# Two steps of the state-space units go from VectorE and GpSimd to ScalarE

## The chip, the cores and the metric

The kernel runs on one core of one Trainium2 chip, as one program. The metric is device microseconds of that core for one execution. Times in the traces are microseconds from the start of the span unless a duration is marked ns. Engines are named as the profile names them: PE (TensorE matmul), PEld (its weight loads), DVE (VectorE), ACT (ScalarE), POOL (GpSimd), SP (the queue that issues most of the transfers).

## The reference, cut to what matters

One layer over 1024 latent tokens and 256 context tokens: a token mixer (differential attention beside a bidirectional Mamba-2 scan, merged by gates), then a mixture of experts. The change touches only the scan. In its chunked form, for one direction:

```python
acum = jnp.cumsum(dtc * a, axis=2)
seg = acum[:, :, :, None] - acum[:, :, None]
decay = jnp.where(lower, jnp.exp(jnp.where(lower, seg, 0.0)), 0.0)
cb = jnp.einsum('bcign,bcjgn->bcijg', cc, bc)
y_diag = jnp.einsum('bcijg,bcijgr,bcjgr,bcjgrp->bcigrp', cb, decay, dtc, xc)
y_off = jnp.einsum('bcign,cbgrpn,bcigr->bcigrp', cc, h_prev, jnp.exp(acum))
```

The kernel does both directions together with chunks of 128 tokens. For each head it needs a matrix W of 128 rows (j) by 128 columns (i) for each chunk: the mask "j up to i" times dt forward plus the mask "j from i" times dt backward, times exp of the smaller of the two differences of the running sums, times the product of B and C.

## The kernel before, in words

The program is built in stages: norm and attention's projections (to about 390 us), the mixer `mixer_t` (about 390 to 1050), attention with the branch products in its gaps, the merge, the experts. A planner written in the kernel (`Flow`) sets the order of all instructions of PE, DVE, ACT and POOL. Each piece of work is a generator (a stream) with a priority, lower first; at each `yield` it names what it needs next: tiles, free buffers of a ring, and the engine whose planned clock must be reached (`wake`, L294). Where no engine is named, the engine is PE. The planner charges a cost for each instruction and hands it to its engine in the order in which streams wake. The engines then run their queues in order and wait for each other by semaphores.

In the mixer, `server` (L945, priority 3) feeds PE with the projections: for each output tile of 128 channels ("job") it multiplies split weights `hi`, `lo` with the normalised tokens into `acc` banks, and goes back to the planner after nine matmuls of 512 columns or at a job's end (six more). Jobs are dt, convolution inputs, z and 16 gate tiles; gate tiles need no scan and are taken when the others can't run. `mixer_load` (L777) fetches a job's weights, ACT casts them to `hi`, DVE subtracts to `lo`.

`dt_post` (L826) makes `dt` and the running sums `ac` (partition j, by direction, chunk and head), and stores their rows to DRAM (`acd`). For each of four head groups, `group` (L990) makes transposes, the `states` of both directions (L1048), and four pairs of units. A **unit** (L1078) is one head over half of the tokens (four chunks); a pair is two heads of the same half. The unit fetches rows of `acd` into two tiles R (one per direction, broadcast over partitions), gets a G and a W buffer, and then:

- DVE: W = mask le times dt, four instructions of 128 by 128 (`F.ts`, one scalar by partition); then W = mask ge times the other dt plus W, four more (`F.stt`)
- POOL: G = R[0] minus the column of `ac`, one instruction of 128 by 512 (`F.ptt`), after R[0] has landed
- DVE: G = min(R[1] minus its column, G), four instructions
- `decays` (L1127): ACT takes exp of R[0] and R[1] in place, POOL multiplies each by C
- POOL: W = W times the product of B and C (`CB`); ACT: exp of G; DVE: W = W times G

`products` (L1111) waits until both units of a pair are planned and their tiles are 400 ns old, then gives PE the matmuls of both heads into `py`, and frees R and W. The rings hold six R, two G and two W. So both W of a pair are in use until its products ran, and the next pair's units start then; one unit's R are fetched ahead, the other's when the products free theirs. After the fourth pair `norm` (L1151) normalises the group's output and stores it (`yn`).

When the fourth group is done, the branch products (`branches`, L1194) open: they load `yn`, and attention's first tiles (`qk`) are fetched once no job is left and five operands are in. Both must come before attention's first matmuls (`sps`).

Of the kernel before, what the change touches and what calls it, by code (L numbers as in the profile page):

```python
# [13 lines left out]
AF = mybir.ActivationFunctionType  # L14
ALU = mybir.AluOpType
# [4 lines left out]
P = 128  # L20
# [354 lines left out]
class Layer:  # L375
# [413 lines left out]
    def mixer_t(s):  # L789
        tc, nc, I, F = s.tc, s.nc, s.I, s.F  # L790
# [9 lines left out]
        if True:  # L800
# [15 lines left out]
            Gs = s.ring(sp, [P, 4, P], "G", 2)  # L816
            Ws = s.ring(sp, [P, 4, P], "W", 2)
            dcol, db = s.dcol, s.db
            dtn = mp.tile([P, 2, 10, 32], F32, name="dtn")
            dt, dtd = dtn[:, 0], dtn[:, 1]  # L820
            ac = mp.tile([P, 2, 10, 16], F32, name="ac")
            cdec = mp.tile([P, 10, 2, 16], F32, name="cdec")
            wst = mp.tile([P, 10, 2, 16], F32, name="wst")
            state = {"dt": False, "conv": {}, "z": set(), "groups": 0, "served": False}

            def dt_post(banks):  # L826
                yield [db, "ACT"]
                F.act(db[:, 1], db[:, 1], AF.Exp)
                yield [aux]
                pt = aux.get()  # L830
                for b, t0, n in zip(banks, (L, L + 512, 0), (512, 512, L)):
                    yield [b, Gs, "ANY"]
                    q = Gs.get()
                    qv = q.rearrange("p a b -> p (a b)")
                    F.copy(qv[:64, :n], b[:64, :n])
                    acc.put(b)
                    yield [q]
                    for i in range(n // P):
                        c = t0 // P + i
                        F.mm(pt[:, c * 32:(c + 1) * 32], q[:64, i], s.fold[:64], True, True)  # L840
                    Gs.put(q)
                yield [pt, db, (Gs, 2), "DVE"]
                tiles = Gs.get(), Gs.get()
                u, e = (q.rearrange("p a b -> p (a b)")[:, :320] for q in tiles)
                F.tt(u.rearrange("p (c h) -> p c h", h=32), pt[:, :320].rearrange("p (c h) -> p c h", h=32), db[:, 0:1].to_broadcast([P, 10, 32]), ALU.add)
                aux.put(pt)
                yield [u, "ACT"]
                F.act(e, u, AF.Abs)
                F.act(e, e, AF.Exp, scale=-1.0)
                F.act(e, e, AF.Ln, bias=1.0)  # L850
                yield [e, "DVE"]
                F.stt(dt.rearrange("p c h -> p (c h)"), u, 0.0, e, ALU.max, ALU.add)
                Gs.put(*tiles)
                yield [dtn, "DVE"]
                F.stt(dtd, dt, -1.0, db[:, 1:2].to_broadcast([P, 10, 32]), ALU.mult, ALU.mult)
                for d, tri in ((0, s.le), (1, s.ge)):
                    yield [dtn, aux]
                    pa = aux.get()
                    F.mm(pa[:, :160].rearrange("p (c h) -> p c h", h=16), tri, dtd[:, :, d * 16:(d + 1) * 16], True, True)
                    yield [pa, "DVE"]  # L860
                    F.vcopy(ac[:, d].rearrange("p c h -> p (c h)"), pa[:, :160])
                    aux.put(pa)
                yield [aux]
                pt = aux.get()
                F.mm(pt[:, :320], s.ones, dtd.rearrange("p c h -> p (c h)"), True, True)
                yield [pt, "ACT"]
                F.act(cdec.rearrange("p c d h -> p (c d h)"), pt[:, :320], AF.Exp)
                yield [ac, "DVE"]
                F.tt(wst, pt[:, :320].rearrange("p (c d h) -> p c d h", d=2, h=16), ac.rearrange("p d c h -> p c d h"), ALU.subtract)
                aux.put(pt)  # L870
                wf = wst.rearrange("p c d h -> p c (d h)")
                yield [wst, "ACT"]
                F.act(wf.rearrange("p c h -> p (c h)"), wf.rearrange("p c h -> p (c h)"), AF.Exp)
                yield [wst, "DVE"]
                F.tt(wf, wf, dt, ALU.mult)
                for d, tri in ((0, s.le), (1, s.ge)):
                    for half in range(2):
                        yield [aux]
                        pa = aux.get()
                        for c in range(4):  # L880
                            F.mm(pa[:16, c * P:(c + 1) * P], dtd[:, 2 + half * 4 + c, d * 16:(d + 1) * 16], tri, True, True)
                        yield [pa, Gs, "DVE"]
                        q = Gs.get()
                        qv = q.rearrange("p a b -> p (a b)")
                        F.vcopy(qv[:16], pa[:16])
                        aux.put(pa)
                        F.dma(s.acd[d][:, half * 512:(half + 1) * 512], qv[:16])
                        Gs.put(q)
                state["dt"] = True
# [55 lines left out]
            def server():  # L945
                box = s.mbox
                nxt = pick()
                while nxt:
# [35 lines left out]
                    if kind == "dt":  # L984
                        F.spawn(0, dt_post(banks))
                    elif kind == "conv":
                        F.spawn(0, conv_post(q, v, 0 if q >= 12 else L, banks))
                state["served"] = True

            def group(g, x0, x1, B, C):  # L990
# [40 lines left out]
                for pair in range(2):  # L1031
                    for half in range(2):
                        yield [pys]
                        py, ready = pys.get(), []
                        for hh in range(2):
                            yield [(Rs, 2), "NOW"]
                            F.spawn(0, unit(g, pair, half, hh, CB, C, ready))
                        F.spawn(1, products(g, pair, half, xn, hp, py, done, ready, yt))
# [39 lines left out]
            def unit(g, pair, half, hh, CB, C, ready):  # L1078

                r = 2 * pair + hh  # L1080
                h = 4 * g + r
                t0 = 512 * half
                R = [Rs.get(), Rs.get()]
                for d in range(2):
                    F.dma(R[d], bass.AP(tensor=s.acd[d].tensor, offset=s.acd[d].offset + h * T + t0, ap=[[0, P], [1, 512]]))
                Rv = [q.rearrange("p (c i) -> p c i", i=P) for q in R]
                yield [Gs, Ws, "DVE"]
                G, W = Gs.get(), Ws.get()
                cs = range(4 * half, 4 * half + 4)
                for c in range(4):  # L1090
                    F.ts(W[:, c], s.le, dt[:, 2 + cs[c], h:h + 1], None, ALU.mult)
                for c in range(4):
                    F.stt(W[:, c], s.ge, dt[:, 2 + cs[c], 16 + h:16 + h + 1], W[:, c], ALU.mult, ALU.add)
                yield [R[0], "POOL"]
                F.ptt(G, Rv[0], ac[:, 0, 2 + 4 * half:6 + 4 * half, h:h + 1].to_broadcast([P, 4, P]), ALU.subtract)
                yield [G, R[1], "DVE"]
                for c in range(4):
                    F.stt(G[:, c], Rv[1][:, c], ac[:, 1, 2 + cs[c], h:h + 1], G[:, c], ALU.subtract, ALU.min)
                k = []
                F.spawn(0, decays(R, C[:, t0:t0 + 512], k, F.clk["DVE"] + 100.0))  # L1100
                yield [CB, W, "POOL"]
                F.ptt(W, W, CB[:, 4 * half:4 * half + 4], ALU.mult)
                yield [G, "ACT"]
                F.act(G, G, AF.Exp)
                yield [G, "DVE"]
                F.tt(W, W, G, ALU.mult)
                Gs.put(G)
                yield [lambda: len(k) == 2]
                ready.append((hh, W, *R))
# [17 lines left out]
            def decays(R, C, k, at):  # L1127
                for q in R:
                    yield [q, at, "ACT"]
                    F.act(q, q, AF.Exp)  # L1130
                    yield [q, "POOL"]
                    F.ptt(q, q, C, ALU.mult)
                    k.append(1)
# [1344 lines left out]
```

## Time and profile before

| | |
|---|---|
| median of three runs | 2810.9 us (2809.32 to 2814.49) |
| profiled execution | 2803.03 us, span 2801.1 us |
| PE busy in the span | 2618.4 us, 93% |
| DVE, ACT, POOL busy | 2008.3, 1339.9, 888.9 us |

The profile was taken from one execution. "Busy" counts the time in which an engine had at least one instruction running; an instruction that is held up inside counts as busy, with a longer duration. A granted clock of 1.00 is TensorE's upper level of 2.4 GHz, and a stretch at the lower one (1.2 GHz) shows as a mean below 1.

### The profile page before, as it was taken

The page shows a single profiled execution, that of the slowest core. Times are in us where ns is not written, and L with a number is a line of the kernel's source. Part 1 is how long each engine was busy: PE and PEld are TensorE (multiplying, and loading weights), DVE is VectorE, ACT ScalarE, POOL GpSimd, SP SyncE. Part 2 cuts the span into 40 slices and gives each one's busy share as a digit, 9 for nine tenths or more (in the row PEclk, how much of TensorE's full clock was granted, in tenths as well). Part 3 has the DMA queues.
Part 4 walks back from the last instruction along what each step waited for, and adds up shares of the span by engine and source line. Part 5 has one row for each costly group of instructions (what it writes and reads, how often), then busy time and mean ns, then how long its engine had stood idle before and what let it go on. Part 6 is the DMA issues. An engine that isn't in the chain of part 4 may idle for free. (4 is left out here: it accounts for less than half of the span.)

```text
span 2801.1 us, 41274 instructions
## 1 busy us (share of the span) xinstructions
PE 2618.4 (93%) x14561; PEld 2101.6 (75%) x14561; DVE 2008.3 (72%) x4690; ACT 1339.9 (48%) x2104; POOL 888.9 (32%) x671
## 2 busy tenths in 40 slices
PE   7999999999999999999999999899999998999891
PEld 4888778778787777888887787688878776776660
DVE  6877123768686749888894767877888877788753
ACT  4211123344444546666764422345666665666641
POOL 0111010545353520000000000065666656567641
PEclk9999999999999999999999999999999999999995
DMA  7767253243334354233234953478899999999997
GB/s 279 221 208 214 67 142 105 67 137 91 121 91 132 106 168 149 81 106 131 88 101 135 292 181 142 170 265 248 293 311 315 312 275 278 301 315 315 317 305 202
DMA packets 275123, 544.63 MB, mean 194 GB/s; under 512 B 31531, under 2 KB 166804, under 8 KB 247907
## 3 DMA queue, kind: packets, MB, share of 16 engines
q1 hardware_dynamic: 238754, 435.05, 45.5%
q0 software_dynamic: 36160, 106.93, 15.1%
q8 instruction: 115, 1.88, 0.3%
q14 instruction: 94, 0.76, 0.1%
HBM read 432.73 MB, written 124.73 MB: 199 GB/s over the span
## 5 line engine op out<-in xcount | busy, mean ns | idle before, releaser
L170 DVE TENSOR_TENSOR gl<-raw,gh 128x1024 fp32r<-128x1024 f32 x240 | 288.1, 1218 | 39.4 <-ACT gh L163 39.4
L147 PE MATMUL acc<-hh,hi 128*128 128x512 f32 (+2 forms) x760 | 304.8, 401 | 1.3 <-DVE ux L186 1.3
L163 ACT CAST gh<-raw 128x1024 fp32r<-128x1024 f32 x240 | 247.5, 1050 | 95.7 <-PE gu L147 63.2
L147 PE MATMUL acc<-hl,hi 128*128 128x512 f32 (+2 forms) x760 | 289.4, 381 | 0.0
L147 PE MATMUL acc<-hh,lo 128*128 128x512 f32 (+1 forms) x736 | 281.0, 382 | 3.0 <-DVE lo L170 3.0
L147 PE MATMUL gu<-gh,xh 128*128 128x512 f32 (+3 forms) x672 | 279.5, 416 | 3.3 <-ACT xh L163 3.0
L147 PE MATMUL gu<-gl,xh 128*128 128x512 f32 (+3 forms) x672 | 265.6, 395 | 4.5 <-DVE gl L170 4.4
L147 PE MATMUL gu<-gh,xl 128*128 128x512 f32 (+3 forms) x672 | 265.7, 395 | 0.5 <-DVE xl L170 0.5
L192 DVE TENSOR_SCALAR_CACHE_REDUCE e<-sps 128x512 f32<-128x512 f32 (+1 forms) x384 | 214.4, 597 | 29.5 <-PE sps L147 29.2
L261 POOL DMA_INDIRECT cr<-cumd,crow x98 | 118.9, 1213 | 312.5 <-DVE crow L186 280.9
L267 POOL DMA_INDIRECT yacc<-y,tk x98 | 184.4, 1881 | 84.5 <-issue 31.4
L147 PE MATMUL sps<-qk 128*128 128x512 f32 (+1 forms) x768 | 195.3, 386 | 8.2 <-DVE e L192 4.8
L155 ACT ACTIVATE e<-e,st 128x1280 f32<-128x1280 f32 x128 | 174.8, 1366 | 31.7 <-DVE st L201 31.5
L261 POOL DMA_INDIRECT wc<-wtab,tk x98 | 143.7, 1466 | 137.7 <-DVE tk L181 101.1
L147 PE MATMUL acc<-hi,hh 128*128 128x512 f32 x448 | 181.1, 404 | 0.0
L147 PE MATMUL acc<-hi,hl 128*128 128x512 f32 x448 | 176.1, 393 | 0.4 <-DVE hl L170 0.4
L147 PE MATMUL acc<-lo,hh 128*128 128x512 f32 x448 | 175.8, 392 | 0.0
L147 PEld LDWEIGHTS sps<-qk 128*128 128x128 f32 x768 | 140.9, 191 | 40.8 <-DVE e L192 9.8
L147 PEld LDWEIGHTS acc<-hh,hi 128*128 128x128 f32 (+1 forms) x760 | 142.5, 187 | 32.7 <-issue 4.2
L147 PE MATMUL pv<-wr,vv 128*128 128x256 f32 x640 | 164.2, 380 | 0.0
L147 PEld LDWEIGHTS acc<-hh,lo 128*128 128x128 f32 x736 | 138.8, 189 | 32.8 <-DVE lo L170 4.0
L147 PEld LDWEIGHTS acc<-hl,hi 128*128 128x128 f32 (+1 forms) x760 | 142.6, 188 | 27.4 <-issue 0.8
(326 smaller groups left out, 6254.8 us busy)
## 6 DMA issues: line engine op xcount, KB each, us to landing
raw<-in_w_e_gate_dram SPq DMA_DIRECT2D x64, 1024.0 KB, 8.6
raw<-in_w_e_up_dram SPq DMA_DIRECT2D x64, 1024.0 KB, 12.4
draw<-in_w_e_down_dram SPq DMA_DIRECT2D x64, 1024.0 KB, 10.8
qk<-qk POOLq DMA_DIRECT2D x16, 1664.0 KB, 11.1
raw<-in_w_in_dram SPq DMA_DIRECT2D x40, 512.0 KB, 4.7
wada<-in_w_ada_dram SPq DMA_DIRECT2D x32, 512.0 KB, 5.5
R<-acd SPq DMA_DIRECT2D x64, 256.0 KB, 5.3
qk<-sa SPq DMA_DIRECT2D x52, 256.0 KB, 4.0
```

What stands on the lines that cost most here:

```text
L147: s.nc.tensor.matmul(out, l, r, start=start, stop=stop)
L155: s.nc.scalar.activation(out, in_, fn, **kw)
L163: s.nc.scalar.copy(out, in_)
L170: s.nc.vector.tensor_tensor(out, a, b, op=op)
L192: s.nc.vector.tensor_scalar(out, a, s1, None, op0=op0, op1=op1, accum_out=acc)
L261: s.nc.gpsimd.indirect_dma_start(out=out, out_offset=None, in_=table, in_offset=bass.IndirectOffsetOnAxis(ap=idx, axis=0), **kw)
L267: s.nc.gpsimd.indirect_dma_start(out=table, out_offset=bass.IndirectOffsetOnAxis(ap=idx, axis=0), in_=in_, in_offset=None, compute_op=ALU. ...
```

## The change

The first step of W (mask times dt) becomes four ACT instructions of 128 by 128 with the scale by partition. The difference R[0] minus the column becomes four ACT instructions with the bias by partition; the column is negated once for all units by a small DVE instruction in `dt_post`. No engine is named any more where a unit gets its G and W; the order of the unit's steps is: W on ACT, G on ACT after R[0], the second step of W on DVE, and then as before.

```diff
@@ -868,6 +868,8 @@
+                yield [wst, "DVE"]
+                F.ts(ac[:, 0], ac[:, 0], -1.0, None, ALU.mult)
                 wf = wst.rearrange("p c d h -> p c (d h)")
@@ -1084,15 +1086,18 @@
-                yield [Gs, Ws, "DVE"]
+                yield [Gs, Ws]
                 G, W = Gs.get(), Ws.get()
                 cs = range(4 * half, 4 * half + 4)
+                yield [W, "ACT"]
                 for c in range(4):
-                    F.ts(W[:, c], s.le, dt[:, 2 + cs[c], h:h + 1], None, ALU.mult)
+                    F.act(W[:, c], s.le, AF.Copy, scale=dt[:, 2 + cs[c], h:h + 1])
+                yield [R[0], "ACT"]
+                for c in range(4):
+                    F.act(G[:, c], Rv[0][:, c], AF.Identity, bias=ac[:, 0, 2 + cs[c], h:h + 1])
+                yield [W, "DVE"]
                 for c in range(4):
                     F.stt(W[:, c], s.ge, dt[:, 2 + cs[c], 16 + h:16 + h + 1], W[:, c], ALU.mult, ALU.add)
-                yield [R[0], "POOL"]
-                F.ptt(G, Rv[0], ac[:, 0, 2 + 4 * half:6 + 4 * half, h:h + 1].to_broadcast([P, 4, P]), ALU.subtract)
                 yield [G, R[1], "DVE"]
                 for c in range(4):
                     F.stt(G[:, c], Rv[1][:, c], ac[:, 1, 2 + cs[c], h:h + 1], G[:, c], ALU.subtract, ALU.min)
```

## Rows read from the trace of the kernel before

**Rows 1.** The page: busy time, share of the span and instructions of each engine.
```profile
PE 2618.4 (93%) x14561; PEld 2101.6 (75%) x14561; DVE 2008.3 (72%) x4690; ACT 1339.9 (48%) x2104; POOL 888.9 (32%) x671
```
**Rows 2.** Windows: stretch, length, busy PE, PEld, DVE, ACT, POOL (x), clock, DMA share, GB/s.
```profile
500.00:1010.00 510.00, 484.51 (x2814) 400.75 (x2813) 369.94 (x874) 230.85 (x329) 240.84 (x199) 0.98 0.36 107
720.00:730.00 10.00, 7.36 (x57) 6.39 (x56) 6.56 (x9) 6.30 (x10) 4.67 (x4) 0.73 0.22 45
```
**Rows 3.** Waits in 500 to 1010: engine line waited for: us, times, longest.
```profile
PE py L147 <- DVE W L170: 14.1, 8, 2.6
PE py L147 <- POOL R L174: 7.3, 9, 3.3
...
POOL G L174 <- DMA R<-acd: 15.7, 9, 3.9
...
DVE W L179 <- PE py L147: 11.1, 6, 5.2
```
**Rows 4.** Groups by form, 500 to 1010: count, busy us, mean ns, idle before, releaser.
```profile
L186 DVE SCALAR_TENSOR_TENSOR G<-R,ac,G 128x128 f32<-128x128 f32 x128 | 77.9, 670 | 8.4 <-POOL G L174 8.4
...
L179 DVE TENSOR_SCALAR W<-cst,dtn 128x128 f32<-128x128 f32 x128 | 47.7, 434 | 11.1 <-PE py L147 11.1
```
**Rows 5.** Timeline of one pair, DVE: start, us, instructions merged [idle before <-releaser].
```profile
690.72 0.86 DVE L179 TENSOR_SCALAR W<-cst,dtn 128x128 f32<-128x128 f32 x4
...
692.55 1.13 DVE L186 SCALAR_TENSOR_TENSOR G<-R,ac,G 128x128 f32<-128x128 f32 x4
693.60 1.99 DVE L179 TENSOR_SCALAR W<-cst,dtn 128x128 f32<-128x128 f32 x4
...
698.18 5.26 DVE L186 SCALAR_TENSOR_TENSOR G<-R,ac,G 128x128 f32<-128x128 f32 x4 [0.94 <-POOL G L174]
...
704.67 0.68 DVE L170 TENSOR_TENSOR W<-W,G 128x512 f32<-128x512 f32 x1
```
**Rows 6.** The same pair, POOL.
```profile
692.77 2.14 POOL L174 TENSOR_TENSOR W<-W,CB 128x512 f32<-128x512 f32 x1 [3.13 <-DVE W L186]
696.90 1.24 POOL L174 TENSOR_TENSOR G<-R,ac 128x512 f32<-128x512 f32 x1 [1.99 <-DMA R<-acd]
698.10 2.59 POOL L174 TENSOR_TENSOR R<-R,uC 128x512 f32<-128x512 f32 x2
```
**Rows 7.** The same pair, PE: a product that waits for the second W.
```profile
705.40 0.32 PE L147 MATMUL py<-W,xn 128*64 128x128 f32 x1 [2.26 <-DVE W L170]
```
**Rows 8.** ScalarE groups by form, 500 to 1010 (columns as in 4).
```profile
L155 ACT ACT_TABLE_LOAD x50 | 64.2, 1283 | 46.1 <-DVE ux L186 12.2 <-DVE uC L186 10.8 <-DMA gt<-zg 10.5
...
L155 ACT ACTIVATE zg<-acc 128x512 f32<-128x512 f32 x38 | 22.7, 598 | 53.5 <-PE acc L147 40.1 <-issue 11.0 <-DMA gt<-zg 2.1
...
L155 ACT ACTIVATE ux<-acc,vcol 128x512 f32<-128x512 f32 x12 | 8.8, 768 | 4.2 <-PE acc L147 4.2
...
L155 ACT ACTIVATE ux<-acc,vcol 128x256 f32<-128x256 f32 x6 | 3.4, 566 | 8.7 <-PE acc L147 8.7
```
**Rows 9.** Timeline, ACT: two exponentials one behind the other.
```profile
527.36 1.15 ACT L155 ACTIVATE R<-R 128x512 f32<-128x512 f32 x2
```
**Rows 10.** Windows of two pairs, from the end of one's products to the next's.
```profile
690.60:708.90 18.30, 15.56 (x113) 12.86 (x112) 17.36 (x34) 7.75 (x12) 11.44 (x8) 1.00 0.32 88
...
844.40:864.00 19.60, 18.25 (x127) 14.76 (x124) 17.35 (x35) 14.53 (x18) 9.96 (x8) 1.00 0.42 126
```
**Rows 11.** Groups by form, PE, 999 to 1054: what PE does after the last pair.
```profile
L147 PE MATMUL acc<-hh,hi 128*128 128x512 f32 x61 | 24.6, 403 | 0.0
...
L147 PE MATMUL bacc<-bxl,bwh 128*128 128x512 f32 x12 | 4.8, 400 | 0.3 <-DVE bxl L170 0.3
...
L147 PE MATMUL sps<-qk 128*128 128x512 f32 x1 | 0.4, 389 | 0.0
```
**Rows 12.** Timeline, PE: matmuls of a job one behind the other.
```profile
656.30 0.40 PE L147 MATMUL acc<-hh,hi 128*128 128x512 f32 x1
656.53 0.40 PE L147 MATMUL acc<-hl,hi 128*128 128x512 f32 x1
```

## The prediction

> **What bounds the kernel now.** I read the page's busy times first: PE is busy for 93% of the span and no other engine is near it [rows 1]. So an engine that is relieved pays only where PE stands still for it. The change acts in the units, so I took the stretch that holds all sixteen pairs, 500 to 1010, by windows [rows 2]: of 510.0 us PE is busy for 484.5, 25.5 are idle. The mean granted clock there is 0.98, about 10 us of work lost to the lower level (0.02 x 510). The second row is where such a loss lies: ten microseconds with 2.64 idle, at a mean clock of 0.73, between 1.2 and 2.4 GHz. So 35 us is all that any change of the units can win there.
>
> The waits name what PE stands still for [rows 3]: 14.1 us in eight places where products wait for W times G, and 7.3 in nine where they wait for R times C. That is 21.4 of the 25.5, or 1.3 us a pair. Then I read one pair in order of time [rows 5 to 7]. W is free at about 690.6. DVE makes the first unit's W; the second's first step takes 1.99 us where the first's took 0.86, because POOL's W times CB, started at 692.77, lies beside it. POOL's G of the second unit waits for R until 696.90. DVE's last step on that G starts at 698.18 and takes 5.26 us for four instructions that took the first unit 1.13 (692.55), because POOL runs multiplications back to back beside it. The second W is ready at 705.3, and PE, there 2.26 us earlier, waits for it. So DVE and POOL hold each other up, and the second unit ends last. By groups the same shows as means: 434 ns for the first step of W (0.86/4 = 215 undisturbed), 670 for the last of G [rows 4, 5].
>
> **The change part by part.** *Taken from DVE:* 128 first steps of W, 47.7 us as they ran and 128 x 0.215 = 27.5 undisturbed. *Taken from POOL:* 32 differences at about 1.24, 40 us [rows 6]. A pair loses 8 x 0.215 = 1.7 us of DVE and 2 x 1.24 = 2.5 us of POOL at undisturbed prices [rows 5, 6], and since the two hold each other up, up to 4 us of its chain.
>
> *Added to ACT:* 256 instructions of 128 by 128. The trace has none of this shape. Convolution inputs with scale and bias by partition take 768 ns for 512 columns and 566 for 256 [rows 8], 0.79 ns a column, so 465 at 128. They have two pointers; the gate activation without any takes 598 for 512, so a pointer is (768-598)/2 = 85, and one pointer at 128 columns is 380. Back to back, two exponentials span 1.15 us at 0.62 each [rows 9], 0.09 of overlap: 0.29 apart. Ends: 0.215, DVE's price for the same step [rows 5], and 0.566 [rows 8]. I take 0.29, whose rows are the same engine. Eight a unit are 2.3 us of ACT's queue (1.7 to 4.5), 4.6 a pair, 74 us in all. ACT is busy for 7.75 us of an 18.3 us pair and for 14.5 of a 19.6 us pair [rows 10]: idle time covers it, with 0.5 us to spare in the fullest.
>
> *The second unit* waits for R as before: POOL waited for it 15.7 us in nine places [rows 3], now ACT does. A G on ACT takes 4 x 0.29 = 1.2 us against POOL's 1.24 [rows 6], so its last step on DVE can't start earlier than at 698. What changes is what lies beside it: POOL needn't wait for R any more and can do W times CB ahead, so fewer multiplications are left to fall on the 5.26 us. Behind the waiting ACT stand exponentials of the first unit, casts of `hi` and evacuations of `acc`. Who waits for them: POOL's R times C, DVE's `lo`, and PE's next job; one job's weights are always ahead, and a job is 48 matmuls at 0.23 us [rows 12] = 11 us, so a wait of 4 us (3.9 is the longest) stays covered, unless the queue is full. DVE's wait for the products that free W, 11.1 us [rows 3], also moves to ACT. I let the chain shrink from 14.6 us (690.7 to 705.3) to 13.5; ends 12 (two thirds of the 4 us above) and 15.
>
> *Moved:* where the units start. Before, a unit that got its W started as soon as DVE's planned clock allowed. Now the request for G and W names no engine, and the planner takes PE's clock. The products free W just as PE's plan returns to the server, which gives it nine matmuls at once (six at a job's end). The units are so planned 9 x 0.23 = 2.1 or 6 x 0.23 = 1.4 us later; on the chip ACT may start as soon as W is free, but the pair's products stand later in PE's queue, behind that much more projection work. I take 1.75 us a pair (ends: 0, if other streams hold the clock, and 2.5). POOL and ACT lose and gain about as much in the planned order, which I take as nothing (0.5 either way).
>
> *In `dt_post`*: one more DVE instruction on 160 columns, at most the 0.434 of a disturbed one of 128 [rows 4], and the exponential of wst behind it. Units begin a hundred microseconds later: nothing. R's transfers and SP's queue keep their order within a unit: nothing, as long as the units start together.
>
> *The sum.* PE then comes to a pair's products at 14.6 - 2.26 = 12.3 us after W is free, plus 1.75 = 14.1, against a chain of 13.5: most waits go. I keep a quarter of 21.4: -16 us. The lost clock shrinks likewise, with the rare long waits: -7. So PE wins 23 us (8 to 32).
>
> But the units are a chain of their own: W's ring lets no pair start before the last one's products, and groups follow one another. Per pair the chain gets -1.0 (waits) -0.45 (clock) +1.75 = +0.3, +5 us for sixteen. So the win doesn't shorten it; PE only does its gate tiles sooner. After the last product, at 999, PE has 3 x 61 matmuls of jobs left [rows 11], 43 us at 0.23, and 36 matmuls of the branch product, 8.4. They fill the 55 us to attention's first scores at 1054, which wait for norm, `yn`, five operands and `qk`. With 23 + 5 us done earlier, 15 us of jobs are left for a tail that stays about as long (some 4 us less, since norm's matmuls no longer stand behind nine others). PE will stand idle there for some 20 us. Attention starts at 1054 + 5 - 4 = 1055; what is really won is branch product done in the idle tail, the same 36 matmuls once more, 8.4 us off attention's PE work. Net +1 - 8.4 = -7. The profiled execution has 2803.0 (2801.1 of span), the median of the runs is 2810.9, 7.9 above; I forecast against the median: 2810.9 - 7.4 = 2803.5, so 2803.
>
> **The rivals.** *The chain really shortens.* If the later place in PE's queue costs nothing (the end 0), the chain loses 1.0 + 0.45 us a pair, the jobs last to the end and PE's win comes through whole: -24, 2787 (2776 to 2797). For it: 4 us of work leave the pair's slowest engines. Against it: the request without an engine.
>
> *ACT becomes the bound, and the mixer slower.* ACT's fullest pairs have 5.1 us to spare for 4.6 [rows 10], and in them ACT loads tables, 50 of 1283 ns in the stretch [rows 8], which the planner doesn't charge. It decides once ACT's queue holds up the last exponential by more than the 0.6 us that are left between 13.5 and 14.1. One gate tile between (two table loads and 0.6 on ACT) is 3.2 us, so 2.6 us more a pair; in half of the pairs that is 21 us on the chain, and in the tail the jobs run out. Attention starts 21 + 1 later, less the 8.4: +14, 2825 (2815 to 2840). Against it: of the sixteen pairs, whose emptiest and fullest stand in [rows 10], nine have ACT busy for less than 11 us. The Trainium skill, "ScalarE: Activation LUTs", "Rules for kernel authors", says to use VectorE, not ScalarE, for adding and multiplying; the section on what a table load costs states 186 ns + 0.833 a column, 93 more for each pointer and 93 of overlap, by which I work out an estimate of 0.386 us an instruction and 0.293 apart, 75 us in all. The trace speaks neither way yet: its rows agree with these prices, and the step leaves an engine that is held up by POOL, which the rule doesn't weigh; taken alone it makes this rival's time the likely one.
>
> *It changes nothing.* ACT waits for R with the first unit's exponentials behind it, the chain stays at 14.6, the waits stay, and the tail is filled as before: 2811 (2806 to 2816).
>
> **How the numbers follow.** Forecast (2796 to 2811): 0.42, of which two thirds, 0.28, lie more than 0.2% under the median (5.6 us, about what a measurement can tell from no change). Chain shortens: 0.20. ACT the bound: 0.25. No change: 0.13. So faster 0.48, same 0.14 + 0.13 = 0.27, slower 0.25. As both signs hold much, the range reaches from inside the second case to inside the third, 2784 to 2826; the forecast's own is 2796 to 2811.
>
> **What would show it.** In 500 to 1010, the products' waits at 5 us instead of 21.4 and a mean clock of 0.99 or more; DVE's last step of G at a mean under 600 ns instead of 670; ACT's new instructions at about 0.38 us, none stretched; pairs of 18 to 19 us. After the last product, far fewer than 61 x 3 matmuls of jobs, and idle PE before the first scores. I am wrong if the jobs left after the last product are as many as before (the chain shortened), if PE waits for W behind ACT's exponentials of G, or if the pairs grow to 20 us and more.

## The result and the profile after

| | before | after |
|---|---|---|
| median of the runs beside each other | 2810.1 us | 2854.6 us |
| ratio | | 1.0149 [1.0115, 1.0182] |
| profiled execution | 2803.0 us | 2861.0 us |
| last product in `py` ends | 999.1 us | 1041.3 us |
| first scores of attention | 1053.9 us | 1094.8 us |

The change makes the kernel 1.5% slower. 41 us of it arise before attention's first scores. Of the other 17 in the profiled execution, 16 lie after the last scores; a second profile of the changed kernel (after_again, below) lacks them: 1750.2 us from first scores to the end, 1747.2 before. So only the 41 are explained here.

The page after, busy times; then the windows from 500 to the last product's end, before and after (stretch, length, busy PE, PEld, DVE, ACT, POOL, clock, DMA share, GB/s):
```profile
PE 2641.2 (92%) x14561; PEld 2110.5 (74%) x14561; DVE 1975.4 (69%) x4562; ACT 1430.5 (50%) x2374; POOL 831.5 (29%) x639
```
```profile
500.00:999.09 499.09, 473.60 (x2764) 391.75 (x2762) 367.29 (x870) 224.69 (x319) 238.26 (x197) 0.98 0.36 108
```
```profile
500.00:1041.32 541.32, 486.06 (x2779) 399.86 (x2777) 335.39 (x745) 318.22 (x591) 180.04 (x166) 0.95 0.34 100
```
The instruction stream gives PE the same 1416 projection matmuls between the first pair's products and the last's in both kernels (counted in 512 columns here and below; one of 256 counts half). The last product ends 42 us later all the same: the first pair's products start 6.5 us later (541.1, 534.6 before), and the way from there takes 36 us longer. Idle PE grows from 25.5 to 55.3 us, and at a mean clock of 0.95 instead of 0.98 some 27 us are lost to the lower level (1.2 GHz) instead of 10. DVE is busy for 32 us less, POOL for 58 less, as intended; ACT for 94 more (81 in the new steps, 15 in twelve more table loads, a little less elsewhere).

PE's waits in that stretch (us, times, longest), to be set against [rows 3]:
```profile
PE py L147 <- POOL R L174: 15.9, 11, 3.2
PE acc L147 <- DVE ux L186: 15.8, 3, 9.3
PE py L147 <- DVE W L170: 12.8, 4, 7.0
PE acc L147 <- DVE uB L186: 9.3, 2, 5.8
```
The products' waits are 28.7 us instead of 21.4: fewer and longer for W, doubled for R times C, which waits for ACT's exponentials. New are 25.1 us in which PE stands for a projection's bank `acc`, which a convolution (`ux`, `uB`) has not emptied.

ScalarE's groups by form, 500 to 1060, against [rows 8]:
```profile
L155 ACT ACT_TABLE_LOAD x63 | 80.8, 1283 | 46.3 <-PE acc L147 16.5 <-DVE ux L186 12.8 <-DVE uB L186 8.3
L155 ACT ACTIVATE W<-cst,dtn 128x128 f32<-128x128 f32 x128 | 40.4, 390 | 13.6 <-PE py L147 13.6
L155 ACT ACTIVATE G<-R,ac 128x128 f32<-128x128 f32 x128 | 40.4, 390 | 8.8 <-DMA R<-acd 8.8
```
The price of one instruction was right. Where it hurts is seen in one pair. First ScalarE in order of time, then VectorE and PE (start, us, instructions merged, idle before and its releaser):
```profile
723.53 1.28 ACT L155 ACTIVATE G<-R,ac 128x128 f32<-128x128 f32 x4 [0.64 <-DMA R<-acd]
724.83 1.28 ACT L155 ACT_TABLE_LOAD   x1
726.13 0.63 ACT L155 ACTIVATE G<-G 128x512 f32<-128x512 f32 x1
726.66 0.62 ACT L155 ACTIVATE R<-R 128x512 f32<-128x512 f32 x1
727.30 1.28 ACT L155 ACT_TABLE_LOAD   x1
728.59 0.60 ACT L155 ACTIVATE zg<-acc 128x512 f32<-128x512 f32 x1
729.21 1.28 ACT L155 ACT_TABLE_LOAD   x1
730.50 0.63 ACT L155 ACTIVATE R<-R 128x512 f32<-128x512 f32 x1
731.35 1.28 ACT L155 ACT_TABLE_LOAD   x1 [0.21 <-DVE yt L170]
732.64 0.60 ACT L155 ACTIVATE zg<-acc 128x512 f32<-128x512 f32 x1
733.26 1.28 ACT L155 ACT_TABLE_LOAD   x1
734.55 0.63 ACT L155 ACTIVATE R<-R 128x512 f32<-128x512 f32 x1
735.09 0.61 ACT L155 ACTIVATE G<-G 128x512 f32<-128x512 f32 x1
```
```profile
727.47 3.20 DVE L186 SCALAR_TENSOR_TENSOR G<-R,ac,G 128x128 f32<-128x128 f32 x4
...
735.79 1.28 DVE L170 TENSOR_TENSOR W<-W,G 128x512 f32<-128x512 f32 x1 [4.52 <-ACT G L155]
```
```profile
737.13 0.47 PE L147 MATMUL py<-W,xn 128*64 128x128 f32 x1 [7.01 <-DVE W L170]
```
The second G is ready on VectorE at 730.7; its exponential runs at 735.1, because in ScalarE's queue gate tiles stand between the exponentials and each change of function loads a table for 1.28 us. PE waits 7.0 us. Before, ScalarE waited for VectorE at that point (54.2 us for G in the stretch; 19.1 after); now VectorE waits for ScalarE. Its wait for the exponential of G, before and then after:
```profile
DVE W L170 <- ACT G L155: 6.2, 7, 3.0
```
```profile
DVE W L170 <- ACT G L155: 37.6, 18, 4.5
```
At another pair it is a bank (ACT, DVE, PE):
```profile
818.13 2.45 ACT L155 ACTIVATE W<-cst,dtn 128x128 f32<-128x128 f32 x8
820.48 1.43 ACT L155 ACTIVATE ux<-acc,vcol 128x512 f32<-128x512 f32 x2
```
```profile
827.27 1.27 DVE L170 TENSOR_TENSOR W<-W,G 128x512 f32<-128x512 f32 x1 [1.71 <-ACT G L155]
828.46 4.15 DVE L186 SCALAR_TENSOR_TENSOR G<-R,ac,G 128x128 f32<-128x128 f32 x4
832.53 0.74 DVE L186 SCALAR_TENSOR_TENSOR ux<-acc,vcol,ux 128x512 f32<-128x512 f32 x1
```
```profile
835.19 0.80 PE L147 MATMUL acc<-hh,hi 128*128 128x512 f32 x1 [9.34 <-DVE ux L186]
```
ScalarE reads the convolution's bank at 820.5, behind eight new steps; VectorE reads it at 832.5, because the planner put the unit's W times G, which waits for an exponential, and the last step of G ahead of it. Here it is mostly the order of VectorE's queue that holds PE for 9.3 us; ScalarE's lateness has a part only in the 1.7 us for which VectorE waits for the exponential.

### The profile page after: what moved, and what is told of

It is laid out like the page before. It is cut to its first block, busy times and chain, and to the rows that moved or that the text cites. A ratio compares the mean times of both kernels' runs of the same rounds, so it can differ in the third digit from the quotient of the medians.

```text
span 2859.2 us, 41345 instructions
## 1 busy us (share of the span) xinstructions
PE 2641.2 (92%) x14561; PEld 2110.5 (74%) x14561; DVE 1975.4 (69%) x4562; ACT 1430.5 (50%) x2374; POOL 831.5 (29%) x639
## 4 chain that ended last, share of the span: by engine, by line
PE 47%; DMA 12%; DVE 7%; ACT 4%; issue 3%; POOL 1%; SPq 0%; POOLq 0%; ACTq 0%; DVEq 0%
PE gu L147 14%; PE dn L147 8%; PE bacc L147 5%; PE acc L147 5%; PE sps L147 4%; PE pv L147 4%; DMA yacc<-y,tk 3%; PE tr L151 2%; PE xt L151 2%; DMA cr<-cumd,crow 2%; DMA qk<-qk 2%; DMA raw<-in_w_e_gate_dram 2%; DVE gl L170 1%; ACT L155 1%; PE py L147 1%
## 5 line engine op out<-in xcount | busy, mean ns | idle before, releaser
L147 PE MATMUL acc<-hh,hi 128*128 128x512 f32 (+2 forms) x760 | 308.8, 407 | 25.1 <-DVE ux L186 15.8
L147 PEld LDWEIGHTS sps<-qk 128*128 128x128 f32 x768 | 139.1, 189 | 42.3 <-DVE e L192 10.8
```

What stands on the lines that cost most here:

```text
L147: s.nc.tensor.matmul(out, l, r, start=start, stop=stop)
```

## The experiments

"Scores" is the start of attention's first scores in the profile (before: 1053.9), and "old order" means that the instructions of PE, VectorE, ScalarE and GpSimd stand as in the kernel before. The transfers in SP's queue move a little even so, in 4 to 32 of 1160 places between two kernels of one order; what that is worth was not tested. Ratios in round brackets belong to kernels that are read up to the scores alone.

| kernel | what ScalarE gets | order | last product | scores | ratio [95%] |
|---|---|---|---|---|---|
| after_again | the change | its own | 1042.2 | 1095.6 | 1.0151 [1.0125, 1.0177] |
| e1 | W's step | its own | 1030.2 | 1105.8 | 1.0176 [1.0153, 1.0198] |
| e2 | G's step | its own | 1005.6 | 1068.1 | 1.0061 [1.0044, 1.0078] |
| e5 after | the change, few loads | as the change | 1005.1 | 1058.0 | 1.0052 [1.0034, 1.0071] |
| e5 before | few loads | old | 992.2 | 1046.8 | 0.9987 [0.9977, 0.9996] |
| e6 | the change | loads charged | 1034.8 | 1072.4 | 1.0106 [1.0086, 1.0125] |
| e7 | 8 unread a unit | its own | 1053.0 | 1111.5 | 1.0224 [1.0203, 1.0245] |
| e8 | the change | convolutions first | 1030.6 | 1080.2 | 1.0177 [1.0157, 1.0197] |
| e9 | the change, convolutions off it | its own | 1032.4 | 1085.9 | 1.0137 [1.0112, 1.0161] |
| e11 | 4 unread, at W's place | its own | 1006.6 | 1069.8 | 1.0097 [1.0068, 1.0126] |
| e12 | 4 unread, at R's place | its own | 1033.1 | 1096.2 | 1.0154 [1.0128, 1.0180] |
| e13 | nothing; steps removed | its own | 989.0 | 1075.9 | (1.0366) |
| e14 | 8 unread a unit | old | 1026.4 | 1081.2 | 1.0096 [1.0079, 1.0113] |
| e15 | nothing | that of e7 | 1020.4 | 1078.8 | 1.0107 [1.0090, 1.0124] |
| e16 | the change | old | 1015.5 | 1070.3 | 1.0064 [1.0047, 1.0081] |
| e17 | a quarter of the instructions, of 8 columns | as the change | 1034.6 | 1087.9 | (1.0561) |
| e18 | G's step | old | 1006.7 | 1061.5 | 1.0046 [1.0028, 1.0064] |
| e19 | W's step | old | 995.1 | 1049.9 | 0.9978 [0.9964, 0.9991] |

**Is it ScalarE at all?** The kernel before plus eight ScalarE instructions a unit whose result nobody reads (e7):
```diff
+                for c in range(8):
+                    F.act(idle, s.le, AF.Copy, scale=dt[:, 2 + cs[c % 4], h:h + 1])
```


> The kernel before, with eight ScalarE instructions of 128 by 128 more at the start of each unit (mask times dt into a tile that nobody reads): the time that the change puts on ScalarE, without anyone waiting for it; 65 table loads. Theory A (ScalarE's time in its queue is what costs, as its exponentials and evacuations of banks come later): 20 us or more over the kernel before, PE's waits in the units' stretch over 40 us. Rival B (what costs is that VectorE's and GpSimd's steps now wait for ScalarE): under 10 us over it, waits under 32.

PE's waits in e7, 500 to the last product, and ScalarE's new group:
```profile
PE acc L147 <- DVE ux L186: 29.3, 5, 10.5
PE py L147 <- POOL R L174: 14.2, 10, 3.2
PE acc L147 <- DVE uB L186: 12.3, 3, 4.7
```
```profile
L155 ACT ACTIVATE idle<-cst,dtn 128x128 bf16<-128x128 f32 x256 | 102.8, 401 | 7.6
```
Scores come 57.6 us later. With nobody relieved and nobody waiting for the result, the same new waits appear. So added ScalarE work, with the order that the planner makes of it, is enough for such a loss. It is more work than the change adds, though: all 256 write one tile, and all but nine wait by a semaphore for the one before. Eight in a row take 3.44 us (e14, from 722.03) where eight of the change's take 2.45, so they hold ScalarE's queue for 110 us, and are busy for 103 where the change's are for 81. What the relief gives back can't be read from the difference. e11 and e12 put four of the eight at the unit's start, or where the difference stands after R[0] (e12: `yield [R[0], "ACT"]`, then four with R[0] as input):
```diff
+                for c in range(4):
+                    F.act(idle, s.le, AF.Copy, scale=dt[:, 2 + cs[c], h:h + 1])
```


> The kernel before with four ScalarE instructions more at the start of each unit (mask times dt into a tile that nobody reads), half of those of the run with eight, which cost 64 us. If ScalarE's time is the price wherever it stands: about 30 us over the kernel before, and as much as the next run. If the place at the unit's start is what costs (ahead of the convolution's evacuations that are due there): 25 to 45 over, and at least 15 more than the next run.

> The kernel before with four ScalarE instructions more in each unit once R[0] is due (R[0] minus the column into a tile that nobody reads): the same ScalarE time as the run before, in the place of the difference. If time counts and not place: about 30 us over the kernel before. If place: 5 to 15 over, like the run that moves the difference alone (16).

Half of the work cost 15.9 us of scores at the start and 42.3 behind the wait for R, and neither expectation had the later place as the dear one. The planner's orders of the two differ little (33 of PE's 12,723 instructions and 12 of VectorE's 4352 stand elsewhere), so the place explains most of the difference: in e12 ScalarE stands for 40.9 us, in eleven places, waiting for R ahead of instructions that nobody reads.

**The table loads.** Silu and Sigmoid in the mixer's gates and convolutions replaced by Tanh, with and without the change: the order is the same to the instruction, but the program loads tables 6 times instead of 73 and 60.
```diff
-                F.act(v, v, AF.Silu)
+                F.act(v, v, AF.Tanh)
...
-AF.Silu if kind == "z" else AF.Sigmoid
+AF.Tanh
```


> The changed kernel with Tanh in place of Silu and Sigmoid in the mixer's gates and convolution (so those activations are wrong and nothing else): the function shares a table with Exp, 6 table loads remain of 73, and the order on PE, DVE and POOL is the changed kernel's, instruction by instruction. Theory A (ScalarE's queue is the bound because table loads that the planner doesn't charge stand between the exponentials): PE's waits in the units' stretch fall from 55 us to under 20, the last product from 1041 to about 1000, time under 2815. Rival B (the new steps and their waits alone lengthen the pairs, loads or not): waits over 40, last product after 1025, time over 2835. Rival C (the products' later place in PE's order costs the time): the order is the same, so no gain beyond the lost clock, over 2840.

> The kernel before with the same Tanh in place of Silu and Sigmoid, same order of everything else. It says how much the loads cost where ScalarE is half idle. Theory A: little, 2800 to 2808, so that the change on top of it costs under 10 us. Rival B: the two Tanh kernels differ by 30 us or more, as the kernels with loads do.

Without loads the change costs 2811.9 - 2796.7 = 15 us instead of 42, and the products' waits do fall, from 20.2 to 10.3 us; but 18.2 us of waits for `ux` and `uB` are there:
```profile
PE acc L147 <- DVE ux L186: 13.4, 3, 8.0
...
PE acc L147 <- DVE uB L186: 4.8, 2, 3.5
```
In the kernel before the loads cost about 4 us (0.9987). So loads, hidden before, carry some 27 of the 42 us in the changed kernel, where the queue is fuller and the order another. What they don't carry is the banks.

**Repairs in the plan.** e6 charges the planner's ScalarE clock with a load at each change of function. e8 gives the convolutions priority over the units. e9 moves the convolutions' first step to VectorE.
```diff
+        if fn in (AF.Exp, AF.Silu, AF.Sigmoid, AF.Ln, AF.Tanh):
+            if fn != s.table:
+                s.clk["ACT"] = max(s.clk["ACT"], s.now) + 1283.0
+            s.table = fn
...
-                        F.spawn(0, conv_post(q, v, 0 if q >= 12 else L, banks))
+                        F.spawn(-1, conv_post(q, v, 0 if q >= 12 else L, banks))
...
-                    F.act(v[:, t0:t0 + n], b[:, :n], AF.Identity, bias=bb, scale=w1)
+                    F.ts(v[:, t0:t0 + n], b[:, :n], w1, bb, ALU.mult, ALU.add)
```


> The changed kernel with 1283 ns charged in the planner for each change of table, so that the plan knows what ScalarE really does; 67 loads. If the loads cost because the plan doesn't know them, PE's products wait under 12 us (from 29) since the plan puts more projection work ahead of them; the jobs then run out before the last product (none are left in the plan, 58 x 3 in the changed kernel), so PE waits in the tail instead: 10 to 40 over the kernel before. If the loads cost by themselves, wherever they stand, the products still wait 20 us or more.

> The changed kernel with the convolution's stream one priority higher than the units', so that of steps that could be planned at the same moment the convolution's come first. If the planned place of the convolution's steps behind the units' is what holds the banks, the waits for ux and uB fall under 10 us (from 25) and the time is 15 to 30 over the kernel before. If it is only that the chip is later than the plan, nothing changes: 35 to 50 over.

> The changed kernel with the first step of the convolution (scale and bias from the bank) on VectorE instead of ScalarE, 36 instructions. If the waits of projections for ux and uB (25 us in the changed kernel, 31 with W alone on ScalarE) come from ScalarE reaching the bank late, they fall under 8 us and the time by 15 or more against the changed kernel, to 15 to 30 over the kernel before. If they come from VectorE's own queue (its later convolution steps stand behind the units' steps), they stay over 15 us and the time stays 35 to 50 over.

None removes the loss. e8 ends the waits for banks (0.6 us) and lets the products wait 31.7; e9 has 39.3 of products and 8.6 of banks. e6 brings PE's waits to about 21 us, under those before, yet scores are 18.5 us late: its pairs stand 864 projection matmuls apart in twelve gaps, 666 before, and no job is left for the tail. e8 is 49 us slower though its scores are only 26.3 late; what it loses after them was not followed. Moving a wait is not removing it.

**Each half, and the relief alone, in orders of their own.** e1 and e2 keep one half of the change's diff each; e13 takes both steps away and puts nothing on ScalarE, so its W lacks the forward mask's dt and R[0] its column; it is read up to the scores alone.
```diff
-                    F.ts(W[:, c], s.le, dt[:, 2 + cs[c], h:h + 1], None, ALU.mult)
+                    F.stt(W[:, c], s.ge, dt[:, 2 + cs[c], 16 + h:16 + h + 1], s.le, ALU.mult, ALU.add)
...
-                F.ptt(G, Rv[0], ac[:, 0, 2 + 4 * half:6 + 4 * half, h:h + 1].to_broadcast([P, 4, P]), ALU.subtract)
...
-                    F.stt(G[:, c], Rv[1][:, c], ac[:, 1, 2 + cs[c], h:h + 1], G[:, c], ALU.subtract, ALU.min)
+                    F.stt(G[:, c], Rv[1][:, c], ac[:, 1, 2 + cs[c], h:h + 1], Rv[0][:, c], ALU.subtract, ALU.min)
```


> Only the mask times dt goes to ScalarE; the difference stays on GpSimd, the column isn't negated. Theory A: 128 new instructions instead of 256, 58 table loads, nothing on ScalarE waits for R, so ScalarE keeps idle time: waits of PE 20 to 35 us, time 2790 to 2820. Rival B: the start of each unit through ScalarE is what costs: 2830 or more.

> Only the difference goes to ScalarE (the column negated); the mask times dt stays on VectorE ahead of it. Theory A: half of the added ScalarE work, 62 table loads: 2805 to 2830. If ScalarE's wait for R with exponentials behind it is what costs, this part carries most of the 44 us: 2835 or more. If it is the start through ScalarE, it carries little: 2815 or less.

> The kernel before without what the change takes from VectorE and GpSimd, and with nothing on ScalarE instead: the first step of W is left out (the second adds the bare mask) and so is R[0] minus its column (the minimum takes R[0] itself), so W is computed wrongly. It gives the relief alone. By the prediction's terms PE wins 23 us (8 to 32) and the chain shortens too, as nothing is placed later: 20 to 45 under the kernel before. If the relief is worth nothing (the pairs are bound elsewhere), within 10 of it.

> The changed kernel itself, once more beside these on the same chip: 35 to 50 us over the kernel before. The first profile of it lost 16 us in the experts' stage beyond the 41 of the mixer; if that belongs to the change, this profile shows it too (1340 us from attention's last scores to the end, 1325 in the kernel before); if not, 1315 to 1325.

W alone costs 49 us, G alone 16, both 40 to 44: no sum. And e13, with less work and nothing added, starts the scores 22 us late, against its expectation: the planner, which charges a shorter unit, sets 564 projection matmuls instead of 666 into the twelve gaps between pairs of one group, PE waits 39 us in the stretch instead of 25 (29 instead of 21 for the products), and 318 matmuls are left for after the last product instead of 183. So the order that the planner makes can be worth tens of us, and every experiment above but e5 mixes it in.

**Time or order?** e14 issues e7's instructions without charging the planner; e15 charges them and issues none.
```diff
-                    F.act(idle, s.le, AF.Copy, scale=dt[:, 2 + cs[c % 4], h:h + 1])
+                    F.nc.scalar.activation(idle, s.le, AF.Copy, scale=dt[:, 2 + cs[c % 4], h:h + 1])
...
+                    F.op("ACT", 94 + 93 + 0.833 * P, idle, (s.le, dt))
```


> The kernel before with the eight unread ScalarE instructions a unit of e7 (64 of that kernel's additions by time: 256 instructions), which now don't move the planner's clock of ScalarE: the order of all other instructions is that of the kernel before. Attention's first scores come at 1053.9 us in the kernel before and at 1111.5 in e7, whose ratio was 1.022. Theory A (ScalarE's time in its queue is the price): scores at 1095 to 1115, ratio 1.014 to 1.024, new waits of PE for a convolution input's bank (acc for ux) of 15 us or more. Theory B (the price is that the planner, charged with that time, arranges the products and projections differently): scores at 1050 to 1065, ratio 0.998 to 1.005, waits as in the kernel before, since 74 us of instructions fit in ScalarE's idle time.

> The other half: the planner charges ScalarE with the eight instructions a unit, but they are not issued. The order of all instructions is that of e7, and ScalarE has no more to do than before. Theory A: scores at 1046 to 1062, ratio 0.997 to 1.004. Theory B: scores at 1090 to 1115, ratio 1.013 to 1.024. If both halves cost some 25 us each, neither alone is the price.

PE's waits, 500 to 1041, in e14 and then in e15:
```profile
PE py L147 <- DVE W L170: 32.3, 13, 5.6
PE py L147 <- POOL R L174: 4.7, 7, 1.8
...
PE acc L147 <- DVE ux L186: 1.8, 1, 1.8
```
```profile
PE acc L147 <- DVE ux L186: 22.8, 6, 8.6
PE py L147 <- POOL R L174: 9.1, 4, 3.3
PE acc L147 <- DVE uB L186: 8.2, 3, 3.7
```
Both theories fall as single causes: time alone costs 27.3 us, order alone 24.9, together 52.2 of e7's 57.6. They differ in kind. ScalarE's time makes the *products* wait for W, behind the exponentials; the order makes the *projections* wait for banks, with none of the ScalarE instructions added (five more table loads come with it, 65 in the program for 60).

e16 and e17 do the same with the change. e16 issues its instructions in the old order, charged as the old ones; e17 keeps its order and issues 64 ScalarE instructions of 8 columns for the 256 of 128 (the decays use their last column, so it is read up to the scores alone).
```diff
-                    F.ts(W[:, c], s.le, dt[:, 2 + cs[c], h:h + 1], None, ALU.mult)
+                    F.nc.scalar.activation(W[:, c], s.le, AF.Copy, scale=dt[:, 2 + cs[c], h:h + 1])
+                    F._dve(W[:, c], (s.le, dt), 1.92, 1)
...
+                for c in range(4):
+                    F.nc.scalar.activation(G[:, c], Rv[0][:, c], AF.Identity, bias=ac[:, 0, 2 + cs[c], h:h + 1])
+                F.op("POOL", 36 + 2.22 * G.free_size(), G, (Rv[0], ac))
```


> The change's instructions on their new engines, but planned and charged as in the kernel before (W's first step on the planner's clock of VectorE, the difference on that of GpSimd, ScalarE's clock not moved): every PE instruction stands where the kernel before has it, and ScalarE's new instructions stand where the old ones were planned. Theory A: VectorE and GpSimd are relieved as in the changed kernel, ScalarE is loaded as there, so scores at 1070 to 1095, ratio 1.006 to 1.015. Theory B: only the relief is left, scores at 1040 to 1054, ratio 0.992 to 1.000, and this version beats both kernels.

> The changed kernel in its own plan, to the instruction, but of each four ScalarE instructions of 128 by 128 that the change adds one of 8 columns is issued, 64 in all for 256; the second step of W and the last of G read its last column in place of the whole difference, so the decays are wrong from there on, and the run is to be read up to attention's first scores alone. ScalarE is left with about 64 x 0.2 = 13 us in place of the 81 that the 256 were busy. Changed kernel: scores at 1095.6, last product at 1042. Theory A: scores at 1040 to 1060, PE's waits for a convolution input's bank under 8 us (16 to 18 in the changed kernel). Theory B: scores at 1080 to 1100.

PE's waits in e16, and ScalarE's wait for R in e17:
```profile
PE py L147 <- DVE W L170: 23.5, 11, 3.6
PE py L147 <- POOL R L174: 5.6, 10, 1.3
...
PE acc L147 <- DVE ux L186: 1.3, 1, 1.3
```
```profile
ACT G L1097 <- DMA R<-acd: 36.5, 10, 4.6
```
In the old order the change costs 16.4 us, at the low end of theory A. That is 10.9 less than e14, but not the relief's worth: e14 holds ScalarE for 110 us instead of some 80, and it has no wait for R. In its own order with 18 us of new ScalarE time instead of 81 the change still costs 34.0 (theory B), and the rest of the time only 7 more. So 25 us (41 less 16.4) to 34 of the 41 come with the order. The 34 isn't pure: e17 keeps the table loads and the wait for R at the head of ScalarE's queue (36.5 us of it, 8.8 in the changed kernel).

Nor are these shares parts of one sum with those of the loads. Without loads, the same new order with all of the change's instructions starts the scores 11 us later than the old one without loads (e5, 1058.0 and 1046.8), instead of 41. So most of what the new order costs, it costs with table loads standing in ScalarE's queue; neither has a price by itself.

**Which step, in a fixed order?** e18 is e16 with G's part alone, e19 with W's alone (three lines):
```diff
                 for c in range(4):
-                    F.ts(W[:, c], s.le, dt[:, 2 + cs[c], h:h + 1], None, ALU.mult)
+                    F.nc.scalar.activation(W[:, c], s.le, AF.Copy, scale=dt[:, 2 + cs[c], h:h + 1])
+                    F._dve(W[:, c], (s.le, dt), 1.92, 1)
```


> As e16 (the change's instructions, every PE instruction where the kernel before has it), but only the difference goes to ScalarE, in four instructions where GpSimd's one was planned; W's first step stays on VectorE. e16 started attention's scores at 1070.3 us, 16.4 later than the kernel before, at a ratio of 1.0064. If the two halves' prices add, and each adds 128 instructions of ScalarE: scores at 1058 to 1066, ratio 1.002 to 1.005. Rival: the difference, which relieves GpSimd and waits for a transfer, is the cheap half in a fixed order (1048 to 1056, ratio 0.996 to 1.001), and W's first step, for which VectorE waits 30.8 us in e16, is the dear one.

> As e16, but only W's first step goes to ScalarE, where VectorE's was planned; the difference stays on GpSimd. Additive halves: scores at 1058 to 1066, ratio 1.002 to 1.005. Rival (W is the dear half): 1064 to 1074, ratio 1.005 to 1.009. In the planner's own orders W alone cost 49 us and the difference alone 16, both together 42 to 44, so the halves didn't add there; with the order fixed, the two ratios over 1 should add to e16's within their intervals if the order was what kept them from adding.

In e18, a wait of ScalarE and one of VectorE; in e19, the same VectorE wait and PE's:
```profile
ACT G L1097 <- DMA R<-acd: 26.7, 8, 7.3
```
```profile
DVE W L170 <- ACT G L155: 33.9, 18, 4.9
```
```profile
DVE W L170 <- ACT G L155: 11.6, 12, 3.4
```
```profile
PE py L147 <- DVE W L170: 13.3, 9, 2.8
PE py L147 <- POOL R L174: 4.7, 8, 1.2
```
Neither expectation named this: W's step, the dearest alone in its own order (e1), *gains* 0.2% in the old one, and e19 is faster than both kernels (2794.5 us, the kernel before beside it 2799.7). The difference costs: ScalarE waits 26.7 us for R with exponentials behind it, a wait that POOL has in the kernel before [rows 3] with only multiplications behind it. That this wait, and not who is relieved (GpSimd in e18, VectorE in e19), makes the difference between the two was not tested in one order; e11 and e12 speak for it. The two still don't add (-4.0 and +7.6 against +16.4), so the order wasn't all that kept them from adding; why the pair of them is dearer was not settled.

## Why the prediction was wrong

- **What bounds the kernel: right.** All that was lost was lost as idle PE and lower clock in the units' stretch. That 35 us was the most to win stood, as no run won more than some 6; what a change can *lose* there has no such bound, and I set none.
- **Price of the ScalarE steps: right.** 390 ns (I had 380), and 0.29 apart as I had it (eight in 2.45 us: 2.45 less the last one's 0.39, over seven). The estimates worked out ahead from the Trainium skill, "ScalarE: Activation LUTs", "What ACT_TABLE_LOAD costs", 0.386 and 0.293, agree too.
- **"Idle time covers it": the step that failed.** I compared busy time in a pair with the pair's length [rows 10], and put the cost at zero. Even that sum was misread: the second window of [rows 10] starts 1.1 us before the products of the pair ahead end; from 845.5 to 863.6 ScalarE has 3.6 us to spare for my 4.6, not 5.1. But one pair isn't the cause. The queue is served in order, and the idle time lay ahead of the exponentials, where ScalarE waited for VectorE's G; a step put there delays them. In the old order the change's 256 steps cost 16.4 us in spite of the relief: VectorE waits 43.3 us for the exponential of G (6.2 before) and PE 23.5 for W (14.1). 256 unread ones, which hold the queue longer, cost 27.3 (e14). Only W's 128 steps fitted, at a gain (e19). In the changed kernel the table loads, which I knew of and left to the rival, carry 27 of 42 us (e5).
- **"ScalarE waits for R as POOL did": wrong by its cover.** I asked only whether a job was ahead of PE, not what the exponentials behind that wait do to the pair. G's move alone costs 7.6 us in the old order (e18).
- **"Moved": wrong in mechanism.** A request that names ScalarE gives the same instructions in the same order on all four engines, so the missing engine name moved nothing. The order did change, because the planner's ScalarE clock runs ahead, and that costs 24.9 (e15) to 34.0 us (e17, with the relief). My 1.75 us a pair isn't that cost. Between pairs of one group the plan does set more, 726 projection matmuls instead of 666 in twelve gaps, 5 or 1.2 us a gap; but between groups it sets as many fewer, so that the last product stands behind only nine more (2 us). What shows in the traces is banks that come free late.
- **The relief: right in sign, no win by itself.** VectorE's last step of G grew instead of falling under 600 ns (first line below against [rows 4]). It fell so in e6 (535), e13 (542) and e18 (586), none of them faster than the kernel before. That relief is worth something shows in e19 alone, a gain of 0.2% with 128 steps on ScalarE; how much, no run says.
- **The tail: wrong.** 58 x 3 matmuls were left, not 15 us of them; as the text said, that meant my chain was wrong, only in the other direction. Groups of VectorE, 500 to 1041, and of PE, 1041 to 1095 (against [rows 11]):
```profile
L186 DVE SCALAR_TENSOR_TENSOR G<-R,ac,G 128x128 f32<-128x128 f32 x128 | 86.7, 736 | 0.0
```
```profile
L147 PE MATMUL acc<-hh,hi 128*128 128x512 f32 x58 | 23.4, 403 | 0.0
```
- **The rival "ACT becomes the bound"** named the mechanism, gate tiles with two loads between the exponentials, and was too small: 22 us of scores where 41 came. It lacked the banks (25 us of new waits) and the planner's answer; and the time, 2854.6, lay above its range (2815 to 2840) too. The rule cited there, from the Trainium skill's "ScalarE: Activation LUTs", "Rules for kernel authors", gave the right sign for the change; e19 shows its limit, since there a multiplication moved to ScalarE gains 0.2%.

## What to carry to other kernels

Idle time of an engine with an in-order queue is cover only at the place where it lies: ask what stands behind the added instruction, whether it is already waited for, and whether the instruction itself waits for a transfer. Where a planner sets the order from charged costs, a moved step changes every queue; try it once in the unchanged order and once charged without being issued, and time and order come apart, as far as they add. A stand-in that nobody reads must take as long as what it stands for: it must not write the same place each time. A step that waits for a transfer belongs in a queue where nothing urgent stands behind it.

## What the runs showed of the hardware

Two things that I had not expected. A table load of 1283 ns, hidden in the kernel before (60 in the program, about 4 us of its time), becomes dear with the change's 81 us in the same queue and the order that comes with them (loads then carry some 27 us of the loss): its length is the same in both, so the price lies in what stands behind it. And the clock followed the waits: the mean granted clock from 500 to the last product was 0.99 in e19, 0.98 before, 0.95 after and 0.93 in e7, so that in the changed kernel a us of PE's waiting cost about half of another one in lost clock (55.3 idle and 27 lost).
